# Average pooling: the loads, the stores and the scaling change engines

## The chip, the cores and the metric

The kernel runs on one core of a Trainium2 chip. The metric is the device time of one execution in microseconds; the time quoted is the median of several runs. The core has four engines that matter here: VectorE (DVE), ScalarE (ACT), GpSimd (POOL) and SyncE (SP, which only issues transfers). ACT, SP and others hand transfers to queues, and 16 DMA engines carry them out.

## What is computed

The input is 32 x 256 rows of 4096 float32 numbers (134.22 MB). Each row is cut into 256 windows of 16 neighbours, and the output (8.39 MB) is the mean of each window:

```python
for i in range(output_size):            # 256
    start = int(i * length / output_size)
    end = int((i + 1) * length / output_size)
    result[:, :, i] = np.mean(x[:, :, start:end], axis=-1)
```

## The kernel before

The 8192 rows go to 128 partitions. There are 16 tiles of 4 rows per partition, each 128 x 16384 numbers (8.39 MB). The first 15 tiles belong to one big group: a partition holds 60 neighbouring rows, and tile t is its t-th block of four. The last tile is a group of its own and is loaded in two halves.

Each tile is loaded into one of two buffers called `xin` (a pool with `bufs=2`). The loads are issued by SP: line 81 for the first 15 tiles, line 89 for the two halves. A load waits for the load that filled its buffer before and for the reading of that buffer by DVE. Ahead of the second load, line 80 has DVE clear part of its buffer; that load waits for this.

The function `pooled` works on a tile, or on a half of the last one. GpSimd takes the second half of the windows and adds the upper 8 numbers of each onto the lower 8, in place (line 66). DVE sums the first half of the windows directly, 16 numbers each (line 69), and then the second half, 8 numbers each, after GpSimd (line 70). The sums go to `res_many` (15 tiles) or `res_last` (the last tile), which stay in on-chip memory to the end. ACT multiplies the finished sums by 1/16 in place (line 73). Its first use of that function loads a table (the row ACT_TABLE_LOAD).

The function `store` (line 58) issues a transfer to the output from ACT, which counts a semaphore `stored` of its own. There are three: all of `res_many` at once (7680 KB), after the last tile's loads are issued in the program and after the scaling of the 15th tile, and then `res_last` in two parts, partitions 0 to 119 and 120 to 127. At the very end SP waits until all three have landed (line 103).

The framework orders each engine's instructions and places the waits; each engine works through its own list in that order. In the list of ACT before: the table load, 15 scalings, the big store, two scalings, two small stores. On SP: the 17 loads and the final wait. On GpSimd: the 17 adds.

Of the kernel before, what the change touches and what calls it, by code (L numbers as in the profile page):

```python
# [1 line left out]

# [4 lines left out]


@with_exitstack
def kernel(  # L10
    ctx: ExitStack,
    tc: tile.TileContext,
    x: bass.AP,
    output_size: int,
    out: bass.AP,
):

    nc = tc.nc
    F32 = mybir.dt.float32
    X = mybir.AxisListType.X

    batch, channels, length = x.shape
    ob, oc, olen = out.shape
    assert ob == batch and oc == channels and olen == output_size
    assert length % output_size == 0
    window = length // output_size  # L30
    hw = window // 2
    inv_w = 1.0 / float(window)

    P = nc.NUM_PARTITIONS
    R = 4
    rows = batch * channels
    assert rows % (P * R) == 0
    ntiles = rows // (P * R)
    many = (ntiles - 1) * R
    cells = R * output_size  # L40
    m = cells // 2
    cols = R * length

    xr = x.rearrange("b c l -> (b c) l")
    orow = out.rearrange("b c o -> (b c) o")
    x_many = xr[0 : P * many, :].rearrange("(p r) l -> p (r l)", p=P, r=many)
    o_many = orow[0 : P * many, :].rearrange("(p r) o -> p (r o)", p=P, r=many)
    x_last = xr[P * many :, :].rearrange("(p r) l -> p (r l)", p=P, r=R)
    o_last = orow[P * many :, :].rearrange("(p r) o -> p (r o)", p=P, r=R)

    res_many = nc.alloc_sbuf_tensor("res_many", [P, (ntiles - 1) * cells], F32, align_bytes=256)
    res_last = nc.alloc_sbuf_tensor("res_last", [P, cells], F32, align_bytes=256)
    inpool = ctx.enter_context(tc.tile_pool(name="inpool", bufs=2))

    stored = nc.alloc_semaphore("stored")

    def store(out, in_):
        ins = nc.scalar.dma_start(out=out, in_=in_)
        tc.no_tile_sem_insts.add(ins.ins.name)
        ins.then_inc(stored, 16)  # L60

    def pooled(xin, res, base, n):


        k = n // 2
        nc.gpsimd.tensor_add(  # L66
            out=xin[:, k:n, 0:hw], in0=xin[:, k:n, 0:hw], in1=xin[:, k:n, hw:window]
        )
        nc.vector.reduce_sum(out=res[:, base : base + k], in_=xin[:, 0:k, :], axis=X)  # L69
        nc.vector.reduce_sum(  # L70
            out=res[:, base + k : base + n], in_=xin[:, k:n, 0:hw], axis=X
        )
        nc.scalar.mul(  # L73
            out=res[:, base : base + n], in_=res[:, base : base + n], mul=inv_w
        )

    for t in range(ntiles - 1):
        xbuf = inpool.tile([P, cols], F32, name="xin")
        if t == 1:
            nc.vector.memset(xbuf[:, 0:1536], 0.0)  # L80
        nc.sync.dma_start(out=xbuf, in_=x_many[:, t * cols : (t + 1) * cols])
        pooled(xbuf.rearrange("p (o w) -> p o w", w=window), res_many, t * cells, cells)

    half = cols // 2
    xbuf = inpool.tile([P, cols], F32, name="xin")
    for h in range(2):
        nc.sync.dma_start(
            out=xbuf[:, h * half : (h + 1) * half],  # L90
            in_=x_last[:, h * half : (h + 1) * half],
        )
    store(o_many, res_many[:, :])
    for h in range(2):
        xin = xbuf[:, h * half : (h + 1) * half].rearrange("p (o w) -> p o w", w=window)
        pooled(xin, res_last, h * m, m)
    for lo, hi in ((0, 120), (120, P)):
        store(o_last[lo:hi, :], res_last[lo:hi, :])

    ctx.pop_all().close()  # L100
    tc.close()
    tc.compile()  # L102
    nc.sync.wait_ge(stored, 48)
    nc.sync.sem_clear(stored)


# [1 line left out]
_INS = ['x', 'output_size']  # L108
_OUTS = [((32, 256, 256), 'float32')]

_NUMBERS = {'output_size': 256}


# [26 lines left out]
```

## Time and profile before

| | before |
|---|---|
| time, median of 3 runs | 333.52 us (333.38 to 333.53) |
| the profiled execution | 333.36 us |
| its span, first to last instruction | 332.1 us |
| DVE, POOL, ACT busy | 211.1, 139.9, 18.4 us |
| moved in all | 142.61 MB, 429 GB/s over the span |

In the profile, a row of the timeline reads: start and length in us, engine, line, operation, output<-input, shapes, and in brackets how long the engine had been idle and what released it. L66 is line 66 of the kernel. SPq and ACTq rows are the issuing of a transfer; the transfer itself runs later. The DMA row cuts the span into 40 equal slices and gives the busy share of the 16 DMA engines in tenths. q1 is the queue that SP feeds, q10 that of ACT. A queue's row gives the number of its packets, the MB, and its share of the 16 engines' time in the stretch that is shown.

### The profile page before, as it was taken

To read this page: it belongs to the slowest core of one execution; us is meant where nothing else is said; L and a number is where in the kernel's file an instruction comes from. 1 tells how busy PE (TensorE), PEld (TensorE's weight loads), DVE (VectorE), ACT (ScalarE), POOL (GpSimd) and SP (SyncE) were. 2 spreads that over 40 slices of the span, in tenths; PEclk is the share of its full clock that TensorE was granted. 3 is DMA by queue.
4 is the path that set the end of the run, shared out by engine and by line. 5 is a ranking of instruction groups with operands and counts; after the bars stand their busy time and mean duration, and the time that the engine had idled before them with its cause. 6 is when DMAs were issued, how large, how long until landed. Compare 5 with 4: busy or idle time off the path is not lost.

```text
span 332.1 us, 167 instructions
## 1 busy us (share of the span) xinstructions
DVE 211.1 (64%) x35; ACT 18.4 (6%) x18; POOL 139.9 (42%) x21
## 2 busy tenths in 40 slices
DVE  1029396592939669293966929396693929569770
ACT  1000101001010100101010010101000010100100
POOL 0028091542809154270916427090642709068050
DMA  9898999989898998989899998989899898989997
GB/s 379 379 497 387 482 403 411 474 379 505 379 497 387 458 426 379 505 379 497 387 482 403 395 489 379 505 379 497 387 450 434 379 505 379 497 383 430 442 466 307
DMA packets 2743, 142.61 MB, mean 429 GB/s; under 512 B 311, under 2 KB 311, under 8 KB 439
## 3 DMA queue, kind: packets, MB, share of 16 engines
q1 hardware_dynamic: 2448, 134.22, 93.6%
q10 hardware_dynamic: 295, 8.39, 5.9%
HBM read 134.22 MB, written 8.39 MB: 429 GB/s over the span
## 4 chain that ended last, share of the span: by engine, by line
DMA 62%; POOL 20%; DVE 10%; issue 3%; POOLq 1%; ACT 0%
DMA xin<-in_x_dram 62%; POOL xin L66 20%; DVE res_many L70 9%; POOLq L102 1%; DVE res_last L70 1%; DVE xin L80 0%; ACT res_last L73 0%; POOLq L66 0%
## 5 line engine op out<-in xcount | busy, mean ns | idle before, releaser
L66 POOL TENSOR_TENSOR xin<-xin 128x4096 f32<-128x4096 f32 (+1 forms) x17 | 139.7, 8216 | 179.7 <-DMA xin<-in_x_dram 179.7
L69 DVE TENSOR_REDUCE res_many<-xin 128x512 f32<-128x8192 f32 x15 | 130.3, 8686 | 105.2 <-DMA xin<-in_x_dram 105.2
L70 DVE TENSOR_REDUCE res_many<-xin 128x512 f32<-128x4096 f32 x15 | 66.3, 4419 | 2.4 <-POOL xin L66 2.3
L73 ACT ACTIVATE res_many<-res_many 128x1024 f32<-128x1024 f32 x15 | 15.8, 1056 | 289.9 <-DVE res_many L70 289.9
L69 DVE TENSOR_REDUCE res_last<-xin 128x256 f32<-128x4096 f32 x2 | 8.8, 4414 | 2.1 <-DMA xin<-in_x_dram 2.1
L70 DVE TENSOR_REDUCE res_last<-xin 128x256 f32<-128x2048 f32 x2 | 4.6, 2280 | 0.1
L80 DVE MEMSET xin<- 128x1536 f32 x1 | 1.3, 1338 | 1.1 <-PEq L121 1.1
L73 ACT ACTIVATE res_last<-res_last 128x512 f32<-128x512 f32 x2 | 1.3, 629 | 13.7 <-DVE res_last L70 13.7
L73 ACT ACT_TABLE_LOAD x1 | 1.3, 1283 | 0.7 <-PEq L121 0.7
L121 POOL MEMSET const-float32-0.0<- 128x1 f32 x1 | 0.1, 98 | 0.2 <-issue 0.2
L121 POOL MEMSET const-bfloat16-1.0<- 128x1 bf16 x1 | 0.1, 101 | 0.0
L121 POOL MEMSET const-uint8-127<- 128x1 uint8 x1 | 0.1, 101 | 0.0
L121 POOL MEMSET const-float32-1.0<- 128x1 f32 x1 | 0.1, 98 | 0.0
## 6 DMA issues: line engine op xcount, KB each, us to landing
xin<-in_x_dram SPq DMA_DIRECT2D x2, 4096.0 KB, 21.6
out_dram<-res_many ACTq DMA_DIRECT2D x1, 7680.0 KB
out_dram<-res_last ACTq DMA_DIRECT2D x1, 480.0 KB
xin<-in_x_dram SPq DMA_DIRECT2D x15, 25.3
out_dram<-res_last ACTq DMA_DIRECT2D x1, 32.0 KB
```

The lines of the kernel that those rows point to most:

```text
L66: nc.gpsimd.tensor_add(out=xin[:, k:n, 0:hw], in0=xin[:, k:n, 0:hw], in1=xin[:, k:n, hw:window])
L69: nc.vector.reduce_sum(out=res[:, base : base + k], in_=xin[:, 0:k, :], axis=X)
L70: nc.vector.reduce_sum(out=res[:, base + k : base + n], in_=xin[:, k:n, 0:hw], axis=X)
L73: nc.scalar.mul(out=res[:, base : base + n], in_=res[:, base : base + n], mul=inv_w)
L80: nc.vector.memset(xbuf[:, 0:1536], 0.0)
L102: tc.compile()
L121: nc = _bacc.Bacc("TRN2", target_bir_lowering=False, num_devices=1)
```

## The change

The three stores are issued by SP, the 17 loads by ACT. The multiplication by 1/16 moves from ACT to GpSimd, so that ACT computes nothing and its list holds no table load.

```diff
     def store(out, in_):
-        ins = nc.scalar.dma_start(out=out, in_=in_)
+        ins = nc.sync.dma_start(out=out, in_=in_)
...
-        nc.scalar.mul(
-            out=res[:, base : base + n], in_=res[:, base : base + n], mul=inv_w
+        nc.gpsimd.tensor_scalar_mul(
+            out=res[:, base : base + n], in0=res[:, base : base + n], scalar1=inv_w
         )
...
-        nc.sync.dma_start(out=xbuf, in_=x_many[:, t * cols : (t + 1) * cols])
+        nc.scalar.dma_start(out=xbuf, in_=x_many[:, t * cols : (t + 1) * cols])
...
     for h in range(2):
-        nc.sync.dma_start(
+        nc.scalar.dma_start(
             out=xbuf[:, h * half : (h + 1) * half],
             in_=x_last[:, h * half : (h + 1) * half],
         )
```

The order of the engines' lists after the change: on ACT the 17 loads; on SP the three stores and the final wait; on GpSimd, for each of the first 14 tiles its add and then its scaling, then the add of the 15th tile, the add of the last tile's first half, the scaling of the 15th tile, the scaling of the first half, the add of the second half and its scaling. DVE's list is the same.

## The prediction

> **What bounds the kernel now.** I read the page first, then the chain of waits, then the timeline of one middle tile and of the tail, then the DMA queues of two stretches of the tail. All durations come from the one profiled execution: span 332.1 us, 1.26 us around it (333.36), 0.16 us under the median of 333.52. A difference of under 0.2% (0.67 us) is about what a measurement of this kernel can't tell from none, and that is the bound that I use.
>
> The page, its first parts:
>
> ```profile
> DVE 211.1 (64%) x35; ACT 18.4 (6%) x18; POOL 139.9 (42%) x21
> ...
> DMA  9898999989898998989899998989899898989997
> ...
> q1 hardware_dynamic: 2448, 134.22, 93.6%
> q10 hardware_dynamic: 295, 8.39, 5.9%
> HBM read 134.22 MB, written 8.39 MB: 429 GB/s over the span
> ```
>
> No compute engine is busy two thirds of the time. The DMA row stays at eight and nine tenths to the last slice, and q1 (the loads) and q10 (the stores) take 99.5% of what 16 engines could give. The trace's records of single transfers say it more sharply. A 65,536-byte piece of a load takes 2.42 us, each beginning where the one before it ended, on all 16 engines, from 2.07 us (first byte) to 331.94 us (last semaphore). On each engine that is 15 x 8 such pieces and 16 of half the size (309.5 us), 8 store pieces of 61,440 bytes at 2.27 us (18.1) and 8 of 4,096 at 0.16 (1.3): 328.9 of these 329.9 us. So the end moves only if the first byte moves, the engines run dry, or a piece takes longer.
>
> The timeline of a middle tile shows what could make them run dry:
>
> ```profile
> 177.61 8.72 POOL L66 TENSOR_TENSOR xin<-xin 128x4096 f32<-128x4096 f32 x1 [10.59 <-DMA xin<-in_x_dram]
> 186.36 4.42 DVE L70 TENSOR_REDUCE res_many<-xin 128x512 f32<-128x4096 f32 x1 [0.17 <-POOL xin L66]
> 190.81 0.33 SPq L81 DMA_DIRECT2D xin<-in_x_dram  x1
> 190.81 1.06 ACT L73 ACTIVATE res_many<-res_many 128x1024 f32<-128x1024 f32 x1 [18.25 <-DVE res_many L70]
> 196.78 8.69 DVE L69 TENSOR_REDUCE res_many<-xin 128x512 f32<-128x8192 f32 x1 [6.00 <-DMA xin<-in_x_dram]
> ```
>
> The buffer comes free when L70 ends (190.78), and the next load is issued at once, while the load before it still runs until 196.76. Each load waits in the queue about 6.0 us before its turn: the lead. The chain of waits calls this a chain of DMA 62%, POOL 20%, DVE 10%, but its POOL and DVE pieces are that buffer's release, 6 us ahead of need. The scaling (ACT L73) is on no path here.
>
> The tail:
>
> ```profile
> 303.22 4.45 POOL L66 TENSOR_TENSOR xin<-xin 128x2048 f32<-128x2048 f32 x1 [1.02 <-DMA xin<-in_x_dram]
> 306.57 4.41 DVE L69 TENSOR_REDUCE res_last<-xin 128x256 f32<-128x4096 f32 x1
> 306.69 1.06 ACT L73 ACTIVATE res_many<-res_many 128x1024 f32<-128x1024 f32 x1 [18.26 <-DVE res_many L70]
> 307.78 0.38 ACTq L58 DMA_DIRECT2D out_dram<-res_many  x1
> ...
> 322.12 0.63 ACT L73 ACTIVATE res_last<-res_last 128x512 f32<-128x512 f32 x1 [8.29 <-DVE res_last L70]
> 322.78 1.04 ACTq L58 DMA_DIRECT2D out_dram<-res_last  x2
> ```
>
> The big store is issued at 307.78, but the transfers show its first piece only at 312.25, in the very place where the last load's pieces stop. It then runs, 8 pieces on each engine, to 330.4. The queues of 312.24 to 330.36 us:
>
> ```profile
> q10 hardware_dynamic: 153, 7.05, 89.8%
> q1 hardware_dynamic: 15, 0.00, 0.0%
> ```
>
> q1 has nothing left in this stretch but 15 semaphore writes. The small last stores, issued at 322.78, stand behind the big store until 330.4. So both stores have slack: the big one some 2.5 to 3 us, the last ones several.
>
> **The change, part by part.**
>
> *The loads go to ACT.* 17 issues of 0.33 to 0.43 us leave SP for a queue that now holds nothing else: the 17 scalings and the three stores are gone from ACT, so no load stands behind anything but its own waits, which are the same (the buffer's earlier load, and L70 or the memset L80). 15 of the 17 have their 6 us lead (the second is issued at 2.49 and needed at 21.9), against which ACT's own issue row (0.38 us, 307.78) and SP's (0.33) differ by nothing. Only the first counts. SP issues it at 0.74 and its first byte moves at 2.07, 1.33 us later. ACT also leaves the opening barrier at 0.74: there its table load starts now, and that is gone. ACT's path from issue to first byte is not shown, because its store had to queue. The nearest row is the store's arrival: from 309.71, 1.93 us after its issue, the loads' pieces stretch from 1.21 to 1.31 us. Bounds: 0 and 0.60 us later; something sooner isn't excluded, and by the spread of these records I allow 0.2. I take 0, since the 1.33 is a first byte and the 1.93 only a first trace of contention.
>
> *Rate of the queues.* The loads take the other queue. In the trace q1 moves 65,536 bytes in 2.418 us and q10 61,440 in 2.267: both 27.1 GB/s an engine. Cost 0.
>
> *The table load goes.* 1.28 us of ACT, from 0.74 to 2.02, with ACT's first use at 36.19: hidden before, worth 0.
>
> *GpSimd scales, middle tiles.* The order of instructions on GpSimd becomes add of tile t, scaling of t, add of t+1. The scaling waits for L70, and the add of the next tile is queued behind it. Its size, 128x1024 in place, isn't in the trace. From below, ACT's 1.06 us; from above, the two-input add's 8.72 us / 4096 = 2.13 ns an element, so 2.18 us. From L70's end at 190.78 it ends by 193.0, and tile t+1 lands at 196.76: 3.7 us to spare. Cost 0. If that cover were gone, L70 and the buffer's release come later, against the 6.0 us lead. So a scaling must exceed 6 us to delay an add and about 12 us to dry out a load.
>
> *GpSimd scales, the tail.* Here the order differs: the last half-tile's first add (303.22 to 307.67) stands ahead of the scaling of tile 14, which was free to start at 306.69. So it starts at 307.7 and ends, by 2.18 us, at 309.9 (by 1.06, at 308.8). I take the upper value for the sum, since that row is GpSimd's own. SP has nothing ahead of the store and issues it 0.03 us later, as ACT did: at 309.9, 2.1 us late. Who waits: with 1.33 to 1.93 us to its first byte it is there at 311.2 to 311.8, and the engines are busy with the last load until 312.25. Cost 0; 0.4 to 1.0 us of slack remain (1.5 to 2.1 at the lower price).
>
> By the Trainium skill (GPSIMD Engine Reference, Elementwise — side-by-side cycle accounting) a one- or two-operation body runs at 1.03 cycles an element at 1.2 GHz, which would be an estimate of 0.88 us here, and about 2.6 cycles for two inputs; 4096 x 2.6 / 1.2 GHz is 8.9 us, and the trace has 8.72. By that page the store would be issued at 308.6, and the cost is again 0.
>
> *The last half.* The next scaling (half the size, at most 1.09 us) waits for L70 at 313.2 and ends at 314.3. The second add follows it in GpSimd's queue. Should its data land at 315.2 as before, it isn't touched; if it lands sooner, the add starts at 314.3. At the latest, then, L70 ends at 322.1 as before, the scaling at 323.2 and SP issues both last stores by 324.3, with their bytes ready by 326.2, against 330.4. Cost 0. The pieces stretched by 0.1 us (two on each engine) may stay or go: 0 to -0.2.
>
> Sum: 333.36 + 0 for the profiled execution, with unknowns from -0.4 to +0.6 us; beside the median, 333.5.
>
> **The rivals.**
>
> *Slower: the big store comes too late and the engines run dry.* The place is 312.25 us. The store has to be issued by 310.3 to 310.9, so this decides from a scaling of 2.6 to 3.2 us, above which each us is a us of the end. If GpSimd takes twice the add's time per element, 4.36 us, the store is issued at 312.1, moves at 313.4 to 314.0, and the time is 334.7 to 335.3. For it: the row is missing, and the add stands ahead. Against: a scaling reads one input where the add reads two. 8%.
>
> *Slower: ACT's queue starts or feeds the loads worse.* The 0.60 us above, with ACT's longer issue (0.38 to 0.58 us against 0.36), makes 0.6 to 0.8: 334.1 to 334.3. For it: no load has run from ACT here. Against: equal rates, equal moment of release. Over the 0.2% in about 7%.
>
> *Faster: the opening was held by the table load.* It ends at 2.02 and the first byte moves at 2.07; the first pieces take 2.90 to 3.63 us against 2.42. If the one causes the other, up to 0.5 to 1.2 us go: 332.3 to 333.0. Against: 14 later tiles begin with full queues, so nothing in the trace tells a cold start from a disturbed one, and SP's issue at 0.74 with 1.33 us to the first byte explains it alone. 12%.
>
> *The change frees nothing that matters, and adds nothing: the forecast.* 73%. That the table load stays in place is not among them: it isn't in the new instruction list.
>
> **How the numbers follow.** 333.5 is the likeliest case. Faster by over 0.2% 0.12, same 0.73, slower 0.15 (0.08 + 0.07). The forecast's own range is 332.9 to 334.1. To 8 in 10 it takes in part of the others: 332.8 below (the milder half of the opening rival), and 334.6 above (all of the late start, and the edge of the late store).
>
> **What would show it.** In the new profile: first load ACTq at about 0.74, first byte near 2.1; a GpSimd L73 row of 1.0 to 2.2 us; load lead 6 us as before; DMA row at eight and nine tenths to the end; big store issued from SP at 308.6 to 309.9 and the last at 322 to 324, ACT with no busy time. The second half may land anywhere from 313.0 to 315.2, with no effect. I would be wrong if the DMA row has a gap near 312 us, if the first byte moves by more than 0.6 us, or if a load's 65,536 bytes no longer take 2.42 us.

## The result, and the profile after

The kernel became slower: 334.54 us (334.38 to 335.58, 7 runs) against 333.52 (333.35 to 333.62, 7 runs). The ratio is 1.0039, 95% interval 1.0027 to 1.005; it takes in all runs, so it isn't the quotient of the medians (1.0031). The forecast was "no change", with "slower" at 15%. Five of the seven runs lie between 334.38 and 334.61, two at 335.6. The profiled execution took 334.54, with a span of 333.2 us.

The page, the parts that answer to those of before:

```profile
DVE 211.1 (63%) x35; POOL 184.3 (55%) x38
...
DMA  9898989999898989899898989899898989899997
...
q10 hardware_dynamic: 2448, 134.22, 93.2%
q1 hardware_dynamic: 295, 8.39, 6.1%
```

ACT has no row any more, GpSimd has 44 us more of work, and the queues have changed places. The DMA row shows nothing of the loss: 1 us is an eighth of a slice.

A middle tile, from the timeline:

```profile
190.45 0.33 ACTq L81 DMA_DIRECT2D xin<-in_x_dram  x1
190.51 2.77 POOL L73 TENSOR_SCALAR res_many<-res_many 128x1024 f32<-128x1024 f32 x1 [4.54 <-DVE res_many L70]
196.41 8.69 DVE L69 TENSOR_REDUCE res_many<-xin 128x512 f32<-128x8192 f32 x1 [5.99 <-DMA xin<-in_x_dram]
196.52 8.72 POOL L66 TENSOR_TENSOR xin<-xin 128x4096 f32<-128x4096 f32 x1 [3.25 <-DMA xin<-in_x_dram]
```

Nothing is lost here. The load is issued 0.06 us ahead of the scaling, the lead is still 6.0 us, and GpSimd is idle for 3.25 us before the next add. The transfers' times from here on are those of their own records, on the clock on which the profile puts them beside the timeline. The prediction had set them by the moment at which VectorE starts on a landed tile, and so had them 0.34 us too late: the kernel before moves its first byte at 1.73 us, not 2.07, ends its last load from 311.91, not 312.25, and writes its last semaphore at 331.60, not 331.94. (Its slack isn't touched by this, as the store's way, the time from its issue to its first piece, and the load's end shift together. The 0.34 us is what lies between the record of a load's semaphore write and the waiting engine's start; whether it is the way of a count or a shift between two clocks isn't shown.) In the kernel after the first byte moves at 1.73 too, and the last load's pieces begin to end at 311.82. Up to there nothing is lost.

The tail, from the timeline:

```profile
302.95 4.45 POOL L66 TENSOR_TENSOR xin<-xin 128x2048 f32<-128x2048 f32 x1 [1.02 <-DMA xin<-in_x_dram]
...
307.48 2.77 POOL L73 TENSOR_SCALAR res_many<-res_many 128x1024 f32<-128x1024 f32 x1
310.28 0.40 SPq L58 DMA_DIRECT2D out_dram<-res_many  x1
...
312.82 4.41 DVE L69 TENSOR_REDUCE res_last<-xin 128x256 f32<-128x4096 f32 x1
...
321.41 1.49 POOL L73 TENSOR_SCALAR res_last<-res_last 128x512 f32<-128x512 f32 x1 [2.41 <-DVE res_last L70]
322.93 1.41 SPq L58 DMA_DIRECT2D out_dram<-res_last  x2
```

The big store is issued at 310.28 instead of 307.78. The single transfers show what that does. Before, all its pieces of 61,440 bytes took 2.27 us. After, its first pieces start at 311.82, just where the load ends, so no engine stands empty for more than 0.1 us, but 13 of the 16 engines need 3.0 to 3.4 us for their first one. The big store's end (the middle one of 16 engines) moves from 330.21 to 330.88, and the last semaphore from 331.60 to 332.72. The small last stores, issued at 322.93, still stand in the queue for 7.3 us and more, until the big store's first engine is done at 330.23.

### The profile page after: what moved, and what is told of

It reads as the page before. It is cut to its first block, busy times and chain, and to the rows that moved or that the text cites. A ratio compares the mean times of both kernels' runs of the same rounds, so it can differ in the third digit from the quotient of the medians.

```text
span 333.2 us, 166 instructions
## 1 busy us (share of the span) xinstructions
DVE 211.1 (63%) x35; POOL 184.3 (55%) x38
## 4 chain that ended last, share of the span: by engine, by line
DMA 60%; POOL 23%; DVE 13%; issue 1%; POOLq 0%
DMA xin<-in_x_dram 60%; POOL xin L66 22%; DVE res_many L70 11%; DVE res_last L69 1%; DVE res_last L70 1%; POOLq L102 0%; POOL res_last L73 0%; POOLq L66 0%
## 5 line engine op out<-in xcount | busy, mean ns | idle before, releaser
L73 POOL TENSOR_SCALAR res_many<-res_many 128x1024 f32<-128x1024 f32 x15 | 41.5, 2768 | 63.7 <-DVE res_many L70 63.6
L70 DVE TENSOR_REDUCE res_many<-xin 128x512 f32<-128x4096 f32 x15 | 66.3, 4420 | 2.5 <-POOL xin L66 2.3
L73 POOL TENSOR_SCALAR res_last<-res_last 128x512 f32<-128x512 f32 x2 | 3.0, 1488 | 5.1 <-DVE res_last L70 5.1
L70 DVE TENSOR_REDUCE res_last<-xin 128x256 f32<-128x2048 f32 x2 | 4.6, 2282 | 1.8 <-POOL xin L66 1.8
```

The lines of the kernel that those rows point to most:

```text
L70: nc.vector.reduce_sum(out=res[:, base + k : base + n], in_=xin[:, k:n, 0:hw], axis=X)
L73: nc.gpsimd.tensor_scalar_mul(out=res[:, base : base + n], in0=res[:, base : base + n], scalar1=inv_w)
```

## The experiments

Theory A: the loss comes from the big store's lateness, and the lateness from the 15th tile's scaling, which is long and stands behind the first half's add. Theory B: the swapped queues cost it. C and D are named where they are tested. "Lead" is the time from the issue of the big store to the first of the 16 engines that ends its last load, both read from the profiled execution of each kernel.

**Which part of the change.** The kernel before with GpSimd's scaling alone:

```diff
-        nc.scalar.mul(
-            out=res[:, base : base + n], in_=res[:, base : base + n], mul=inv_w
+        nc.gpsimd.tensor_scalar_mul(
+            out=res[:, base : base + n], in0=res[:, base : base + n], scalar1=inv_w
         )
```

> The kernel before with one part of the change: GpSimd scales; SP still issues the loads and ACT the stores. Theory A (the late big store: 15th tile's scaling of 2.77 us stands behind the first half's add, so the store is issued at about 310.3 us and its first pieces are stretched by about 1 us): the whole loss is here, 334.3 to 334.7, first store pieces of 3.0 to 3.4 us. Theory B (the swapped queues cost it): 333.4 to 333.6, first store pieces of 2.27 us.

334.66 us (334.39 to 335.62), ratio 1.0035 (1.0023 to 1.0048). Its timeline:

```profile
307.43 2.77 POOL L73 TENSOR_SCALAR res_many<-res_many 128x1024 f32<-128x1024 f32 x1
310.23 0.38 ACTq L58 DMA_DIRECT2D out_dram<-res_many  x1
```

The queues are those of before, and the whole loss is there, with first store pieces of 3.1 us (the middle one of 16 engines). B is out. The other half of the test keeps the swapped queues and makes the store early: the kernel after, scaling on VectorE.

```diff
-        nc.gpsimd.tensor_scalar_mul(
+        last = nc.vector.tensor_scalar_mul(
...
-        pooled(xin, res_last, h * m, m)
+        with tc.issue_after(last.ins):
+            pooled(xin, res_last, h * m, m)
```

> The kernel after with the scaling on VectorE, the 15th tile's scaling directly behind its sums, so that the queues stay swapped but the big store is issued at about 307 us. Theory A: the loss is gone, 333.3 to 333.6, first store pieces of 2.27 us. Theory B: 334.4 to 334.6 as after.

333.60 us (333.40 to 333.79), ratio 1.0003 (0.9994 to 1.0011). The store is issued at 308.07, 1 us later than I had expected (the last section has the likely reason), with 3.8 us of lead, and its pieces take 2.27 us. The swap costs nothing that can be measured.

**Only the 15th tile.** The kernel after with that one scaling moved to ACT:

```diff
+        if on_act:
+            nc.scalar.mul(
+                out=res[:, base : base + n], in_=res[:, base : base + n], mul=inv_w
+            )
+            return
         nc.gpsimd.tensor_scalar_mul(
...
+        pooled(xbuf.rearrange("p (o w) -> p o w", w=window), res_many, t * cells, cells,
+               on_act=(t == ntiles - 2))
```

> The kernel after with the scaling of the 15th tile alone on ACT, behind the load issues; GpSimd scales the 14 tiles before it and both halves of the last. The big store is issued from SP at about 307.7 us. Theory A: the loss is gone, 333.3 to 333.6; GpSimd's other 16 scalings cost nothing. Theory D (GpSimd's scalings slow the loads or the last half): 334 or more.

333.59 us (333.51 to 333.69), ratio 1.0004 (0.9995 to 1.0013). From its page and its timeline:

```profile
DVE 211.1 (64%) x35; ACT 2.3 (1%) x2; POOL 181.6 (55%) x37
```

```profile
306.27 1.06 ACT L74 ACTIVATE res_many<-res_many 128x1024 f32<-128x1024 f32 x1 [17.19 <-DVE res_many L70]
307.35 0.39 SPq L58 DMA_DIRECT2D out_dram<-res_many  x1
...
321.84 1.49 POOL L78 TENSOR_SCALAR res_last<-res_last 128x512 f32<-128x512 f32 x1 [2.41 <-DVE res_last L70]
323.35 1.12 SPq L58 DMA_DIRECT2D out_dram<-res_last  x2
```

GpSimd still does 181.6 us of work and 16 of the 17 scalings, the last one included, and the small stores are issued later than in any kernel so far. All of that is free. D is out. One instruction of 17 carries the loss.

**The order on GpSimd.** The kernel after, the 15th tile's scaling ahead of the first half's add:

```diff
-        nc.gpsimd.tensor_scalar_mul(
+        last = nc.gpsimd.tensor_scalar_mul(
...
-        pooled(xin, res_last, h * m, m)
+        with tc.issue_after(last.ins):
+            pooled(xin, res_last, h * m, m)
```

> The kernel after with one order changed: on GpSimd the scaling of the 15th tile stands ahead of the add of the last tile's first half. The big store is issued at about 309.2 us in place of 310.3. Theory A: the loss is gone or nearly so, 333.3 to 333.8. Theory B: 334.4 to 334.6. Theory C (the end is set by the scaling of the last half, which GpSimd does later): this order makes the last half later still, by 3 to 4 us, so 335 or more.

```profile
306.45 2.77 POOL L73 TENSOR_SCALAR res_many<-res_many 128x1024 f32<-128x1024 f32 x1 [4.54 <-DVE res_many L70]
309.24 0.40 SPq L58 DMA_DIRECT2D out_dram<-res_many  x1
309.30 4.45 POOL L66 TENSOR_TENSOR xin<-xin 128x2048 f32<-128x2048 f32 x1
```

334.03 us (333.32 to 335.10), ratio 1.0017 (1.0006 to 1.0027): half of the loss, and above the range that I gave A. The single runs are spread over 1.8 us, where those of before lie within 0.6. The profiled one took 333.32, all its store pieces at 2.27 us, with the small stores issued only at 326.10. So C is out: in that execution the last half was 3 us later at no cost. But a store that is only 1.5 us late is not safe either, and A needed a curve.

**The curve.** The kernel before, with nothing changed but k more multiplications of the 15th tile's sums by 1.0 on ACT ahead of the big store (k is 1, 2, 3 or 5):

```diff
+    for _ in range(k):
+        nc.scalar.mul(
+            out=res_many[:, (ntiles - 2) * cells :], in_=res_many[:, (ntiles - 2) * cells :], mul=1.0
+        )
     store(o_many, res_many[:, :])
```

k = 1:

> The kernel before with one more multiplication by 1.0 on ACT ahead of the big store, so it is issued at about 309.0 us, some 3.1 to 3.3 us before the last load's pieces end. Theory A with a knee below 3 us of lead: 333.4 to 333.6, as before. Theory A without a sharp knee (the lead is needed to different lengths from run to run): single runs between 333.4 and 334.5, median 333.6 to 333.9.

k = 2:

> The kernel before with the big store alone made late: two more multiplications of the 15th tile's sums by 1.0 on ACT ahead of it, 2 x 1.06 us, so it is issued at about 309.9 us; queues and engines are those of before. Theory A: 0.4 to 0.9 us slower, 333.9 to 334.4, first store pieces stretched. Theory B: 333.4 to 333.6.

```profile
308.09 2.14 ACT L94 ACTIVATE res_many<-res_many 128x1024 f32<-128x1024 f32 x2
310.26 0.39 ACTq L58 DMA_DIRECT2D out_dram<-res_many  x1
```

This is the plainest test of A: the queues, GpSimd's work and the places of the scalings are those of before, only the store is late, issued at 310.26, and the median is 334.33, 0.8 us more. The store's first pieces, which should have been stretched, took 2.27 us in the profiled execution.

k = 3:

> The kernel before with three more multiplications by 1.0 on ACT ahead of the big store, issued at about 311.3 us, 0.9 us ahead of the last load's end. Between 1.8 us of lead (after, 1.0 slower) and -1.1 us (2.8 slower) a straight line gives 1.6 slower: 334.7 to 335.4. If a store that finds the engines just empty pays a fixed price of about 1 us and nothing more until it misses by more than that: 334.4 to 334.7.

k = 5:

> The kernel before with five more multiplications by 1.0 on ACT ahead of the big store, so it is issued at about 313.4 us, 1.2 us after the last load's pieces end. Theory A: the engines are empty for the whole way of the store; 1.2 us and the 2 to 2.9 us from an issue to full flow, so 336.7 to 337.6. Theory B (lateness of the store doesn't matter): 333.4 to 333.6.

And a cheaper scaling in the place of the dear one: the kernel after, the scaling as a product with a tile of 1/16.

```diff
+    sixteenth = nc.alloc_sbuf_tensor("sixteenth", [P, cells], F32, align_bytes=256)
+    nc.gpsimd.memset(sixteenth[:, :], inv_w)
...
-        nc.gpsimd.tensor_scalar_mul(
-            out=res[:, base : base + n], in0=res[:, base : base + n], scalar1=inv_w
+        nc.gpsimd.tensor_mul(
+            out=res[:, base : base + n], in0=res[:, base : base + n], in1=sixteenth[:, 0:n]
         )
```

> The kernel after with the scaling as a two-input multiplication by a tile filled with 1/16, still on GpSimd and in the same place. If the price goes by element and input as the prediction bounded it, one of 1024 elements takes 2.2 us in place of 2.77, the big store is issued at about 309.7 us, and theory A gives 333.5 to 334.4, between before and after. If the scaling's 2.77 us is what any operation of that size costs on GpSimd, 334.4 to 334.7.

All kernels by the big store's lead. Each ratio is against runs of the kernel before that were taken beside it (their medians are 333.42 to 333.52), and the losses in the text are against the same runs:

| kernel | store issued, us | lead, us | median (all runs), us | ratio to before (95%) |
|---|---|---|---|---|
| 15th tile on ACT | 307.35 | 4.4 | 333.59 (333.51 to 333.69) | 1.0004 (0.9995 to 1.0013) |
| before | 307.78 | 4.1 | 333.52 (333.35 to 333.62) | |
| scaling on VectorE | 308.07 | 3.8 | 333.60 (333.40 to 333.79) | 1.0003 (0.9994 to 1.0011) |
| before, k = 1 | 308.60 | 3.1 | 333.60 (333.32 to 334.39) | 1.0010 (1.0001 to 1.0018) |
| scaling first | 309.24 | 2.5 | 334.03 (333.32 to 335.10) | 1.0017 (1.0006 to 1.0027) |
| two-input scaling | 309.94 | 1.9 | 334.06 (333.41 to 334.49) | 1.0017 (1.0008 to 1.0026) |
| before, k = 2 | 310.26 | 1.8 | 334.33 (333.31 to 335.01) | 1.0019 (1.0009 to 1.0029) |
| after | 310.28 | 1.5 | 334.54 (334.38 to 335.58) | 1.0039 (1.0027 to 1.005) |
| GpSimd's scaling alone | 310.23 | 1.2 | 334.66 (334.39 to 335.62) | 1.0035 (1.0023 to 1.0048) |
| before, k = 3 | 310.83 | 0.8 | 334.41 (334.01 to 334.55) | 1.0027 (1.0016 to 1.0038) |
| before, k = 5 | 313.20 | -1.5 | 336.23 (335.83 to 336.38) | 1.0082 (1.0068 to 1.0096) |

With 3.8 us of lead or more the time is that of before, and all runs agree. From 3.1 to 1.8 us the runs spread: the fastest are as fast as before, the slowest 1 to 1.6 us slower. At 1.5 us and less no run is as fast as before, and the price stays near 1 us down to 0.8. A store that misses the load's end altogether adds to that: 1.8 us more at -1.5. (By the measured leads a straight line from after, 1.0 us slower at 1.5, to k = 5, 2.8 slower at -1.5, gives 1.4 us for k = 3 and not the 1.6 of the expectation. It lost 1.0 in the median and 1.1 at most, so the fixed price holds there.)

The k = 5 kernel also gives the bare way of a store to idle engines, from issue to first piece. DMA row and rate of the stretch 312.9 to 314.5 us, then the issue in its timeline:

```profile
DMA  0000000000000000000000000000099999000000
GB/s 0 0 0 0 0 0 0 0 0 0 0 0 0 0 0 0 0 0 0 0 0 0 0 0 0 0 0 0 0 1536 9216 4608 7680 1536 0 0 0 0 0 0
```

```profile
313.20 0.39 ACTq L58 DMA_DIRECT2D out_dram<-res_many  x1
```

A packet is counted where it starts. Each column is 0.04 us, and the first that isn't empty, the 30th, begins at 314.06; the single transfers put the first piece at 314.10, 0.90 us after the issue. (In the first load that way is 0.99.) These first pieces take 2.30 us. So this store into idle engines starts within a microsecond and runs at nearly full speed (2.30 us against 2.27). In the kernel after it had 1.5 us to the load's end, and was stretched all the same. 336.23 is 0.5 us below the least that theory A had given, since it had reckoned with 2 to 2.9 us for the way.

**Big store or small ones.** In the profile of after, the big store's end is 0.67 us late and the way from it to the last semaphore 0.45 us longer (1.84 against 1.39). Both kernels without the two small stores (their 0.52 MB of the output stay unwritten):

```diff
-    for lo, hi in ((0, 120), (120, P)):
-        store(o_last[lo:hi, :], res_last[lo:hi, :])
...
-    nc.sync.wait_ge(stored, 48)
+    nc.sync.wait_ge(stored, 16)
```

> The kernel before without its two small last stores (0.52 MB of the output are left out; the sums and scalings stay). It gives the base for the next kernel: the time ends with the big store, some 1.3 us sooner, 332.0 to 332.3, single runs within 0.4 us.

> The kernel after without its two small last stores (0.52 MB of the output left out). In the profile of after the big store ends 0.6 us later than before, and the small stores take 0.45 us longer. If both parts are real: 0.5 to 0.8 us above the kernel before without small stores, so 332.6 to 333.0. If the whole loss is in the big store's late first pieces: 0.9 to 1.2 us above it. If it is all in the small stores: 0 to 0.2.

332.16 us (332.07 to 332.44) and 333.02 (332.69 to 333.65): 0.86 us apart, where the whole kernels are 1.02 apart. That lies between two of the readings, both parts real (0.5 to 0.8) and the big store alone (0.9 to 1.2). Most of the loss is made by the big store, and the 0.16 us that is left for the small ones is within the spread of these runs.

## Why the prediction was wrong

**The middle tiles, the table load, the queues: right.** The first byte moves at 1.73 us as before, a load's 65,536 bytes still take 2.42 us, the lead is 6.0 us, and both swapped queues and 16 scalings are free. The rival of a worse start on ACT's queue and the rival of an opening held by the table load are both refuted: the first pieces still take 2.5 to 3.3 us with the table load gone (2.7 to 3.6 before). The last half's semaphore was full at 312.5, ahead of the foretold 313.0 to 315.2, and VectorE took it up at 312.82, right behind its work before, with no effect. None of the three signs of being wrong appeared: no gap in the DMA row, the first byte in its place, 2.42 us for a load's piece. What grew was the store's pieces, for which the prediction had named no sign.

**The step that failed: the tail's scaling, "Cost 0".** Two terms of it were mis-sized, both toward "hidden", and the second decided. With the measured 2.77 us in the prediction's own sum the store is issued at 310.5, which by its slack costs 0.2 us at most. And the two-input kernel issued its store at 309.94, about the 309.9 of the prediction, and still lost 0.6 us in the median.

*The price of the scaling.* It was bounded from above by the two-input add, 2.13 ns an element, so 2.18 us. The profile of after by shape:

```profile
L73 POOL TENSOR_SCALAR res_many<-res_many 128x1024 f32<-128x1024 f32 x15 | 41.5, 2768 | 63.7 <-DVE res_many L70 63.6
L73 POOL TENSOR_SCALAR res_last<-res_last 128x512 f32<-128x512 f32 x2 | 3.0, 1488 | 5.1 <-DVE res_last L70 5.1
```

2.77 us; from the two sizes, 2.5 ns an element and 0.2 us for each instruction. One input is not cheaper than two. In the two-input kernel:

```profile
L75 POOL TENSOR_TENSOR res_many<-res_many,sixteenth 128x1024 f32<-128x1024 f32 x15 | 35.1, 2338 | 63.5 <-DVE res_many L72 63.5
L75 POOL TENSOR_TENSOR res_last<-res_last,sixteenth 128x512 f32<-128x512 f32 x2 | 2.5, 1263 | 5.7 <-DVE res_last L72 5.7
```

The same product is 0.43 us cheaper with a second tensor in place of the scalar. I took an assumption ("a scaling reads one input where the add reads two") for a bound. The estimate of 0.88 us, worked out from the Trainium skill (GPSIMD Engine Reference, Elementwise — side-by-side cycle accounting), is a third of what was measured, so here the measurement decides. The store was issued at 310.28, past the 309.9 that I called the latest.

*The slack of the store.* "The store has to be issued by 310.3 to 310.9" came from a way of 1.33 to 1.93 us (0.99 to 1.59 by the transfers' own records) and from the picture that a store which arrives by the load's end costs nothing. The way was about right for idle engines: 0.90. The picture was wrong. The kernels that issue between 308.6 and 310.28 should all have been free, and they lost 0.2 to 1.2 us in the median. For no loss in any run the lead has to be over 3.1 us (3.8 is enough), not 1.0 to 1.6. I had read the store's first trace of contention as its arrival, and so as the point up to which lateness was free.

**The rival that came true** was the late store. Its place and its cause (the add that stands ahead on GpSimd) are those of the runs; 8% was too little for it, and its knee of 2.6 to 3.2 us of scaling was set too late. Its effect was another than foretold: the engines did not run dry in the kernel after, the store's first pieces took longer. "Each us is a us of the end" holds only roughly, and only where the store misses the load's end (from 0.8 to -1.5 us of lead, 2.4 us, the time grows by 1.8); before that stands a step of about 1 us. The predicted sign of change was decided by 0.4 to 1.0 us of slack that rested on two unmeasured numbers, and 73% did not say so.

**What stays open.** The trace shows where time is lost, not by what. In after and in the kernel with GpSimd's scaling alone it is the first store pieces; in the profiled executions of k = 2 and k = 3 these take 2.27 and 2.49 us (the middle one), and the way from the big store's end to the last semaphore is 2.8 and 2.5 us instead of 1.39. In the profiles of the three kernels with 3.8 us of lead or more, 9 to 16 of the 16 engines write the last load's semaphore only after the store's first piece, and 11 to 21 of that load's pieces are slowed from 1.21 us to between 1.25 and 1.63: load and store overlap inside the engines. In the other eight of the table every one of these semaphores goes ahead of the store. Whether that overlap is what saves the microsecond in every run wasn't tried; single executions do without it, since the profiled one of "scaling first" has none and took 333.32. Nor do I know why runs of one kernel with 1.8 to 3.1 us of lead differ, or what the two runs of after and the one of GpSimd's scaling alone at 335.6 have in common.

No kernel here beats the one before. The best versions with the new queues equal it.

## What to carry to other kernels

When transfers set the time, look for the place where one queue's work ends and another's begins; the issue of the first transfer of the new queue is on the path there even if the profile shows it waiting in line. Give it several microseconds of lead (here 3.8 us were enough and 3.1 were not in every run), and check what stands ahead of its producer in that engine's list. A slack smaller than the spread of an unmeasured duration is not cover: put the dearer case into the forecast, not only into the range.

## What the hardware showed that I had not expected

On GpSimd the multiplication by a scalar costs more than the product of two tensors of the same shape: 2768 against 2338 ns for 128x1024.

On VectorE the same scaling takes 0.69 us, 14 times of 15. The 15th time it met an add on GpSimd:

```profile
302.05 4.42 DVE L70 TENSOR_REDUCE res_many<-xin 128x512 f32<-128x4096 f32 x1 [0.17 <-POOL xin L66]
303.04 4.45 POOL L66 TENSOR_TENSOR xin<-xin 128x2048 f32<-128x2048 f32 x1 [1.02 <-DMA xin<-in_x_dram]
306.51 1.53 DVE L73 TENSOR_SCALAR res_many<-res_many 128x1024 f32<-128x1024 f32 x1
307.96 4.41 DVE L69 TENSOR_REDUCE res_last<-xin 128x256 f32<-128x4096 f32 x1
308.07 0.39 SPq L58 DMA_DIRECT2D out_dram<-res_many  x1
```

It ends 0.55 us after the add's end at 307.49, so it seems to have waited for the add, while the sum ahead of it (L70) overlaps the same add and takes the 4.42 us that it takes everywhere. That agrees with the Trainium skill (SBUF — State Buffer, Who interferes with whom): a scaling on VectorE can use a second pair of ports that it shares with GpSimd, and then one of the two blocks; a reduction doesn't. It is one case against 14, so the cause is likely and not shown. Without the 0.84 us that the scaling took longer, that store would have been issued at about 307.2 and not at 308.07.
